# Keys of both heads of a forgetting pair turned together, their low parts multiplied over 64 partitions

## The chip, the core and the metric

The kernel runs on one core of a Trainium2 chip. TensorE (PE) multiplies; its weight loads (PEld) have a row of their own in the profile. VectorE (DVE), ScalarE (ACT) and GpSimd (POOL) work on tiles in on-chip memory, and SyncE (SP) issues most transfers. The metric is the time of one execution on the device in microseconds; lower is better.

## The reference

One layer of a hybrid decoder, for 1024 tokens of width 1024 in float32:

```python
xn = rmsnorm(x, attn_norm_g)
proj = jnp.einsum('bsd,de->bse', xn, w_in)
qa, ka, va, qb, kb, vb, f_logit = jnp.split(proj, IN_SPLITS, axis=-1)
...
out_a = swa_sinks_attention(qa, ka, va, sink_logits)     # 8 heads of 64, window 128, 2 key heads
qb = rmsnorm(qb.reshape(b, s, B_HEADS, HEAD_DIM), q_norm_b)
kb = rmsnorm(kb.reshape(b, s, B_HEADS, HEAD_DIM), k_norm_b)
log_f = jax.nn.log_sigmoid(f_logit + b_forget)
out_b = forgetting_attention(qb, kb, vb, log_f)          # 8 heads of 64, causal, logit += c[t] - c[s]
x = x + jnp.einsum('bse,ed->bsd', mixed, w_out)
hn = rmsnorm(x, mlp_norm_g)
x = x + jnp.einsum('bsf,fd->bsd', jnp.square(jax.nn.relu(jnp.einsum('bsd,df->bsf', hn, w_up))), w_down)
```

The change lies in the forgetting attention: the product of queries and keys, before the softmax, for 8 heads in 4 pairs.

## The kernel before

Float32 accuracy is had by splitting. A number is written as a high part, which the array multiplies exactly enough, and a low part, the rest; a product of two such numbers is made of high by high, high by low and low by high, each a matmul of its own. All matmuls go through one helper (line 73), splits through lines 77 to 80.

The program has five stages that overlap at their edges: the first projection (to about 45 us), the windowed attention of the eight a-heads (45 to about 172 us), the forgetting attention of the b-heads (scores from 179 to 410 us), the output projection, and the two large products of the feed-forward part (about 445 us to the end). While attention runs, TensorE is also given the projections of the pairs to come (tile ps) and, later, the output projection (tile po); these "fillers" are put in at fixed counts of finished score units (PACE).

A b-pair p has two heads. Its work is eight units, four for head 0 (units 0 to 3), four for head 1 (4 to 7); a unit takes two blocks of 128 queries, in the order ORDER_B = (0, 2, 1, 3). For each chunk of up to 512 keys, `scores_b` issues three matmuls into a tile spb:

- q1 by k1: over 128 partitions. q1 holds the head's 64 query features twice, the high parts in one half of the partitions and the low parts in the other; k1 holds the high parts of the keys in both halves. So one matmul gives high by high and low by high.
- q1 by k2: k2 has the low parts of the keys in the head's own half (rows 0 to 63 for head 0, 64 to 127 for head 1), and zeros in the other half, so that the low parts of the query add nothing. There are two such tiles, `k2_of[0]` for all heads 0 and `k2_of[1]` for all heads 1; POOL writes the zeros once, in pair 0.
- in the last chunk, the causal mask, a bf16 matmul of a 128x128 identity by the mask.

DVE then adds the bias cb and takes a running minimum (line 663), and ACT takes the exponential (line 669). `mix_b` turns the probabilities (tpb), splits them (pth, ptl) and multiplies by the values (pvb).

Queries and keys come from the projection with tokens on partitions, and are turned on TensorE by `turn` (line 302): four 128-token transposes into one tile of 512 columns. `make_q_b` turns both heads' queries at once (128 columns of features). `make_k_b` turns the keys of one head (64 columns), once for each half c of the tokens; `k_split` then copies them twice into k1 on ACT (lines 343, 344) and subtracts the low parts into k2 on DVE (line 346). The next pair's tiles are prepared during the current pair (`ahead`): queries at unit 4, keys of head 0 at unit 5, values of head 0 at unit 6, keys of head 1 at unit 7.

Buffers of one tag are taken in turn: "q1" has four, "k1" two. A writer waits until the last reader of the tile that had the buffer is done. The a-heads' queries and keys use the same tags before.

Which instruction of several ready ones goes first on an engine is settled when the program is built, by priorities (`prep` raises them) and a simulated timeline; afterwards each engine has a fixed order.

Of the kernel before, what the change touches and what calls it, by code (L numbers as in the profile page):

```python
# [8 lines left out]
F32 = mybir.dt.float32  # L9
F32R = mybir.dt.float32r  # L10
BF16 = mybir.dt.bfloat16
AF = mybir.ActivationFunctionType
ALU = mybir.AluOpType
# [3 lines left out]
P = 128  # L17
D = 1024
S = 1024
KT = D // P  # L20
NT = S // P
HD = 64
# [33 lines left out]
def hybrid_layer(  # L56
# [13 lines left out]
    nc = tc.nc  # L70

    def mm(out, lhsT, rhs, start, stop):
        return nc.tensor.matmul(out, lhsT, rhs, start=start, stop=stop)  # L73
# [8 lines left out]
    def rsqrt(pool, out, t, shape, tag):  # L82
# [15 lines left out]
        out=ident, in_=ident, pattern=[[-1, P]], compare_op=ALU.not_equal,  # L98
# [17 lines left out]
    for i in range(2):  # L116
        nc.vector.tensor_tensor(
            out=gqk[:, i : i + 1], in0=vec[:, 2 * i : 2 * i + 1],
            in1=vec[:, 2 * i + 1 : 2 * i + 2], op=ALU.mult,
# [25 lines left out]
    ap2 = at.enter_context(tc.tile_pool(name="ap2", bufs=1, side="right"))  # L145
# [5 lines left out]
        out=maskd, in_=maskd, pattern=[[-1, P]], compare_op=ALU.is_ge,  # L151
# [23 lines left out]
    for k in range(KT):  # L175
# [10 lines left out]
        for cs in halves:  # L186
            nc.scalar.activation(xh[:, k, cs], xr[:, cs], AF.Copy, scale=ga[:, k : k + 1])
            last_x = nc.vector.scalar_tensor_tensor(
                out=xl[:, k, cs], in0=xr[:, cs], scalar=ga[:, k : k + 1],
                in1=xh[:, k, cs].bitcast(F32), op0=ALU.mult, op1=ALU.subtract,  # L190
# [102 lines left out]
    def q_split(hi, lo, src, gain):  # L293
        nc.scalar.activation(hi, src, AF.Copy, scale=gain)
        nc.vector.scalar_tensor_tensor(
            out=lo, in0=src, scalar=gain, in1=hi.bitcast(F32), op0=ALU.mult, op1=ALU.subtract
        )

    def turn(x, col, w, c, name):
        pt = pa.tile([P, 512], F32, tag="tr", name=name, bufs=3)  # L300
        for j in range(4):
            nc.tensor.transpose(  # L302
                pt[:w, j * P : (j + 1) * P], x[:, 4 * c + j, col : col + w], ident
            )
        return pt
# [3 lines left out]
    def paced():  # L309
        return tc.issue_after(marks[-1]) if marks else nullcontext()  # L310

    qa, va = {}, []
    rows_of = [slice(h * HD, (h + 1) * HD) for h in range(2)]

    def tiles_q_a(g, c):
        for j in range(2):
            qa[g, j, c] = ap2.tile([P, 2, 512], F32R, tag="q1", name=f"q1a{g}{j}", bufs=4)

    def make_q_a(g, c, j):
        x, col = (((q0, 0), (q3, 0)), ((q3, P), (q3, 2 * P)))[g][j]  # L320
# [4 lines left out]
            q_split(q1[r, h, :], q1[ro, h, :], pt[r, :], gqk[r, 0:1])  # L325

    def make_q_b(x, p):
        q1 = [ap2.tile([P, S], F32R, tag="q1", name=f"q1b{p}{h}", bufs=4) for h in range(2)]
        for c in range(2):
            cs = slice(c * 512, (c + 1) * 512)  # L330
            pt = turn(x, 0, P, c, "ptq")
            for h in range(2):
                r, ro = rows_of[h], rows_of[1 - h]
                q_split(q1[h][r, cs], q1[h][ro, cs], pt[r, :], gqk[r, 1:2])
        return q1
# [2 lines left out]

    k2_of = [ap2.tile([P, S], F32R, name=f"k2z{i}") for i in range(2)]

    def k_split(k1, i, src, cs, both):
        r, ro = rows_of[i], rows_of[1 - i]
        nc.scalar.copy(k1[r, cs], src)
        nc.scalar.copy(k1[ro, cs], src)
        for rr in (r, ro) if both else (r,):
            nc.vector.tensor_tensor(
                out=k2_of[i][rr, cs], in0=src, in1=k1[r, cs].bitcast(F32), op=ALU.subtract
            )

    k1a = {}  # L350

    def make_k_a(x, col, c):
        cs = slice(c * 512, (c + 1) * 512)
        pt = turn(x, col, P, c, "ptk")
        for g in range(2):
            if c == 0:
                k1a[g] = ap2.tile([P, S], F32R, tag="k1", name=f"k1a{g}", bufs=2)
            k_split(k1a[g], g, pt[rows_of[g], :], cs, True)

    def make_k_b(x, col, p, h):  # L360
        k1 = ap2.tile([P, S], F32R, tag="k1", name=f"k1b{p}{h}", bufs=2)
        if p == 0:
            nc.gpsimd.memset(k2_of[h][rows_of[1 - h], :].bitcast(F32), 0.0)
        for c in range(2):
            cs = slice(c * 512, (c + 1) * 512)
            pt = turn(x, col + h * HD, HD, c, "ptk")
            k_split(k1, h, pt[:HD, :], cs, False)
        return k1

    def evict_pt(pt, cols):  # L370
        hi = ap2.tile([P, 512], F32R, tag="pth", name="pth", bufs=3)
# [10 lines left out]
    for t in range(NT):  # L382
# [4 lines left out]
        out=rt, in0=rt, scalar1=1.0 / D, scalar2=EPS, op0=ALU.mult, op1=ALU.add  # L387
# [6 lines left out]
    for t in range(0, NT, 4):  # L394
# [8 lines left out]
        out=dist, in_=dist, pattern=[[-1, 256]], compare_op=ALU.is_ge, fill=BIG,  # L403
# [3 lines left out]
        out=dist, in_=dist, pattern=[[1, 256]], compare_op=ALU.is_ge, fill=BIG,  # L407
# [8 lines left out]
    for pattern, base, sign in (  # L416
# [5 lines left out]
            out=before, in_=before, pattern=pattern, compare_op=ALU.is_ge, fill=0.0,  # L422
# [56 lines left out]
    def start_a():  # L479
        for c in range(2):  # L480
            tiles_q_a(0, c)
        for t in range(2):
            wa1_tile(t)
        for c in range(2):
            wa1_tile(2 + c)
            with tc.issue_after(middle[-1]):
                prep(make_k_a, q0, P, c)
            prep(make_q_a, 0, c, 0)
        for g in range(2):
            va.append(split_v(q0[:, :, 256 + g * HD : 256 + (g + 1) * HD], f"va{g}"))  # L490
        prep(make_q_a, 0, 0, 1)
        for t in range(4, NT):
            wa1_tile(t)
        prep(make_q_a, 0, 1, 1)
# [128 lines left out]
    heads = {}  # L623

    def prep_q(p):
        heads[p, "q"] = make_q_b(qkb[p], p)

    def prep_k(p, h):
        heads[p, "k1", h] = make_k_b(qkb[p], P, p, h)
        if h == 0:  # L630
            load_c(p, 0)

    def load_c(p, h):
        cb = heads[p, "cb", h] = ap2.tile([P, S], F32, tag="bias", name=f"cb{p}{h}", bufs=2)
        nc.sync.dma_start(cb, c_d[2 * p + h].partition_broadcast(P))
# [3 lines left out]
        heads[p, "v", h] = split_v(qkb[p][:, :, c0 : c0 + HD], f"vb{p}{h}")  # L639

    def scores_b(p, qp, h):
        q1, k1, k2, cb = heads[p, "q"][h], heads[p, "k1", h], k2_of[h], heads[p, "cb", h]
        probs = []
        for i in (2 * qp, 2 * qp + 1):
            nk = (i + 1) * P
            pr = ap2.tile(
                [P, S if i > 3 else 512], F32, tag="s" if i > 3 else "u", name="sb",
                bufs=NS if i > 3 else NU,
            )
            nm = ap3.tile([P, 4], F32, tag="nm", name="nmb", bufs=4)  # L650
            dn = ap3.tile([P, 4], F32, tag="dn", name="dnb", bufs=4)
            qs = q1[:, i * P : (i + 1) * P]
            for c in range((nk + 511) // 512):
                n = min(512, nk - c * 512)
                ne = max(n, 256)
                ks = slice(c * 512, c * 512 + ne)
                sp = pa.tile([P, 512], F32, tag="sc", name="spb", bufs=2)
                last = (c + 1) * 512 >= nk
                mm(sp[:, :ne], qs, k1[:, ks], True, False)
                mm(sp[:, :ne], qs, k2[:, ks], False, not last)  # L660
                if last:
                    pe = mm(sp[:, n - P : n], ident_b, mask_b, False, True)
                nc.vector.tensor_tensor_reduce(
                    out=pr[:, c * 512 : c * 512 + n], in0=sp[:, :n],
                    in1=cb[:, c * 512 : c * 512 + n], scale=1.0,
                    scalar=3e38 if c == 0 else nm[:, 0:1],
                    op0=ALU.add, op1=ALU.min, accum_out=nm[:, c : c + 1],
                )
            nc.scalar.activation(
                pr[:, :nk], pr[:, :nk], AF.Exp, scale=-1.0, bias=nm[:, c : c + 1],  # L670
                accum_out=dn_b[p % 2][:, h, i : i + 1] if p < 3 else dn[:, 0:1],
            )
            probs.append(pr)
            if p < 3:
                continue
            nc.vector.reciprocal(dn[:, 1:2], dn[:, 0:1])
            if i > 1:
                nc.vector.tensor_scalar_mul(pr[:, :nk], pr[:, :nk], dn[:, 1:2])
            else:
                nc.gpsimd.tensor_tensor(  # L680
                    out=pr[:, :nk], in0=pr[:, :nk],
                    in1=dn[:, 1:2].to_broadcast([P, nk]), op=ALU.mult,
                )
        marks.append(pe.ins)
        return probs
# [46 lines left out]
    qkb = {}  # L732
# [24 lines left out]
    def ahead(p, u):  # L757
        if p > 3:
            return
        if u == 4:  # L760
            prep(prep_q, p)
        if u == 5:
            prep(prep_k, p, 0)
        if u == 6:
            prep(prep_v, p, 0)
        if u == 7:
            prep(prep_k, p, 1)
# [155 lines left out]
    rr = o["zr"].tile([P, S], F32, name="rr")  # L923
# [334 lines left out]
    for i in range(len(STEPS)):  # L1258
        down(i)
        if STEPS[i][0] == len(PHASES) - 1 and late:  # L1260
            name, dt, cs = late.pop(0)
# [63 lines left out]
```

## Time and profile before

| | us |
|---|---|
| median of 3 runs | 1100.29 (1097.19 to 1101.08) |
| profiled execution, its own time | 1097.17 |
| its span | 1095.5 |
| TensorE busy in the span | 1081.4 |
| DVE, ACT, POOL busy | 774.7, 571.6, 365.2 |

The span goes from the first to the last instruction; the profiled execution's own time also holds what lies around it. A matmul's row in the timeline gives its start and its whole latency, and matmuls overlap, so what one costs is the distance from its start to the next one's start, not its length. The same goes for weight loads. A tile named 128*64 in such a row uses 128 rows and 64 columns of the array; the form behind it is the output.

### The profile page before, as it was taken

What the parts mean: (1) busy time and instruction counts of PE and PEld (TensorE: products, weight loads), DVE (VectorE), ACT (ScalarE), POOL (GpSimd) and SP (SyncE); (2) the same over time, 40 slices, a digit from 0 to 9 for tenths busy, and PEclk for the clock granted to TensorE, in tenths of its full rate; (3) what the DMA queues carried; (4) which work ended last, traced back from release to release, by engine and by line L of the source; (5) the groups of instructions that cost most, each with busy time, mean ns of one, the idle gap of its engine ahead of it and who ended that gap; (6) DMA issues with size and microseconds to landing.
All of it is one profiled execution on the core that took longest, in us unless ns stands there. A gap on an engine that the chain in (4) does not pass through costs nothing.

```text
span 1095.5 us, 15678 instructions
## 1 busy us (share of the span) xinstructions
PE 1081.4 (99%) x5557; PEld 934.0 (85%) x5557; DVE 774.7 (71%) x1327; ACT 571.6 (52%) x1013; POOL 365.2 (33%) x352
## 2 busy tenths in 40 slices
PE   9999999999998999999999999999999999999998
PEld 8999999999996888778888888888888888888886
DVE  8377677766777883898686869765665867674395
ACT  5558588676767764554545454443633433333331
POOL 5672523435433564223223232332222222222100
PEclk9999999999999999999999999999999999999999
DMA  8401212334347457663554443344898876665423
GB/s 301 146 23 52 71 38 61 115 93 149 116 154 279 156 174 280 228 214 127 195 194 177 172 165 143 144 173 144 311 391 312 306 288 230 233 224 186 174 91 115
DMA packets 96079, 195.69 MB, mean 179 GB/s; under 512 B 7376, under 2 KB 19584, under 8 KB 96000
## 3 DMA queue, kind: packets, MB, share of 16 engines
q1 hardware_dynamic: 95856, 194.66, 50.9%
q8 instruction: 44, 0.72, 0.3%
q14 instruction: 35, 0.29, 0.1%
q10 hardware_dynamic: 144, 0.02, 0.0%
HBM read 141.61 MB, written 53.04 MB: 178 GB/s over the span
## 4 chain that ended last, share of the span: by engine, by line
PE 86%; DVE 6%; DMA 5%; issue 1%; ACT 1%; POOL 1%; SPq 0%; ACTq 0%; DVEq 0%
PE pd L73 27%; PE pu L73 27%; PE ps L73 13%; PE po L73 5%; PE spb L73 3%; PE pvb L73 3%; PE tpb L705 3%; DMA xr<-in_xT_dram 1%; PE sp L73 1%; PE pv L73 1%; DMA xq<-in_x_dram 1%; PE tpa L534 1%; DMA h_d<-h 1%; PE ptk L302 1%; DVE bl L80 1%
## 5 line engine op out<-in xcount | busy, mean ns | idle before, releaser
L73 PE MATMUL pd<-hx,wx 128*128 128x512 f32 (+1 forms) x1350 | 304.9, 388 | 0.0
L73 PEld LDWEIGHTS pd<-hx,wx 128*128 128x128 f32 x1350 | 252.7, 188 | 52.2
L73 PE MATMUL pu<-bh,wu 128*128 128x512 f32 x896 | 276.5, 390 | 1.1 <-ACT wu L77 1.1
L73 PEld LDWEIGHTS pu<-bh,wu 128*128 128x128 f32 x896 | 168.2, 188 | 36.6 <-ACT wu L77 1.6
L73 PE MATMUL ps<-w,xh 128*128 128x384 f32 (+1 forms) x640 | 176.0, 345 | 0.7 <-DVE z L431 0.6
L73 PE MATMUL pu<-bl,wu 128*128 128x512 f32 x448 | 174.5, 390 | 0.6 <-DVE bl L80 0.6
L77 ACT CAST hx<-hr 128x1024 fp32r<-128x1024 f32 x56 | 58.9, 1052 | 176.6 <-PE pd L73 170.6
L80 POOL TENSOR_TENSOR wx<-wda,wx 128x1024 fp32r<-128x1024 f32 x24 | 64.5, 2686 | 196.4 <-ACT wx L77 169.1
L80 DVE TENSOR_TENSOR hx<-hr,hx 128x1024 fp32r<-128x1024 f32 x56 | 72.3, 1299 | 72.4 <-ACT hx L77 72.4
L73 PEld LDWEIGHTS ps<-w,xh 128*128 128x128 f32 x640 | 115.3, 189 | 3.1 <-DVE z L431 1.0
L73 PE MATMUL ps<-w,xl 128*128 128x384 f32 (+1 forms) x320 | 109.8, 344 | 0.0
L73 PEld LDWEIGHTS pu<-bl,wu 128*128 128x128 f32 x448 | 84.1, 188 | 19.2 <-DVE bl L80 1.0
L73 PE MATMUL po<-mix,wos 128*128 128x512 f32 x384 | 94.0, 395 | 1.0 <-ACT wos L77 0.7
L80 POOL TENSOR_TENSOR wu<-wus,wu 128x512 fp32r<-128x512 f32 x32 | 47.2, 1476 | 127.2 <-ACT wu L77 127.2
L73 PEld LDWEIGHTS po<-mix,wos 128*128 128x128 f32 x384 | 70.4, 188 | 15.5 <-ACT wos L77 1.1
L80 POOL TENSOR_TENSOR wu<-wur,wu 128x512 fp32r<-128x512 f32 x32 | 43.3, 1354 | 88.7 <-ACT wu L77 88.7
L77 ACT CAST wu<-wus 128x512 fp32r<-128x512 f32 x64 | 38.4, 618 | 58.8 <-PE pu L73 55.1
L374 DVE TENSOR_TENSOR ptl<-tpb,pth 128x512 fp32r<-128x512 f32 (+1 forms) x80 | 49.3, 631 | 25.1 <-ACT pth L373 23.1
L999 DVE TENSOR_TENSOR ht<-hb 128x512 f32<-128x512 f32 x32 | 21.8, 722 | 63.2 <-ACT hb L1054 63.2
L80 POOL TENSOR_TENSOR w<-wr,w 128x384 fp32r<-128x384 f32 (+1 forms) x47 | 51.5, 1106 | 41.2 <-ACT w L77 29.3
L77 ACT CAST wx<-wda 128x1024 fp32r<-128x1024 f32 x56 | 58.2, 1044 | 6.7 <-DMA wda<-in_w_d_dram 6.6
L73 PEld LDWEIGHTS ps<-w,xl 128*128 128x128 f32 x320 | 60.3, 188 | 1.0
(214 smaller groups left out, 1935.9 us busy)
## 6 DMA issues: line engine op xcount, KB each, us to landing
wda<-in_w_d_dram SPq DMA_DIRECT2D x34, 1024.0 KB, 9.0
hr<-hid_d SPq DMA_DIRECT2D x56, 512.0 KB, 6.0
wur<-in_w_u_dram SPq DMA_DIRECT2D x32, 512.0 KB, 4.3
hid_d<-ht SPq DMA_DIRECT2D x16, 1024.0 KB, 4.3
hid_d<-hb SPq DMA_DIRECT2D x16, 768.0 KB, 3.6
mix<-mixs_d SPq DMA_DIRECT2D x7, 1024.0 KB, 7.4
wr<-in_w_b_dram SPq DMA_DIRECT2D x32, 192.0 KB, 2.5
xr<-in_xT_dram SPq DMA_DIRECT2D x16, 256.0 KB, 4.8
```

The lines of the kernel that those rows point to most:

```text
L73: return nc.tensor.matmul(out, lhsT, rhs, start=start, stop=stop)
L77: hi_eng.copy(hi, src)
L80: lo_eng.tensor_tensor(out=lo, in0=src, in1=hi.bitcast(F32), op=ALU.subtract)
L302: nc.tensor.transpose(pt[:w, j * P : (j + 1) * P], x[:, 4 * c + j, col : col + w], ident)
L374: nc.vector.tensor_tensor(out=lo[:, cols], in0=pt[:, cols], in1=hi[:, cols].bitcast(F32), op=ALU.subtract)
L534: nc.tensor.transpose(tp[:, hh * P : (hh + 1) * P], pts[hh // 2][:, hh % 2, c0 : c0 + P], ident)
L705: nc.tensor.transpose(tp[:, c0 : c0 + P], probs[qi][:, kb * P : (kb + 1) * P], ident)
L999: eng.tensor_tensor(out=out, in0=a, in1=b, op=ALU.subtract)
```

## The change

For pairs 1 to 3, the keys of both heads are turned together, 128 columns of features at a time, one half of the tokens at unit 5 and the other half at unit 7. Pair 0 keeps one head at a time. The low parts of both heads of a pair now stand in one tile, `k2_of[p % 2]`, head 0 in rows 0 to 63 and head 1 in rows 64 to 127; the zeros are gone, and the q1 by k2 matmul runs over the 64 partitions of the head, for queries and keys alike. The tags "q1" and "k1" are replaced by six named places, q0 to q5, and a table QK says in which places a pair's two query tiles and two key tiles stand.

```diff
+    QK = ((0, 1, 4, 5), (2, 3, 0, 4), (1, 5, 2, 0), (3, 4, 1, 2))
+
+    def qk1(i, shape, name):
+        return ap2.tile([P] + shape, F32R, tag=f"q{i}", name=name, bufs=1)
...
-        q1 = [ap2.tile([P, S], F32R, tag="q1", name=f"q1b{p}{h}", bufs=4) for h in range(2)]
+        q1 = [qk1(QK[p][h], [S], f"q1b{p}{h}") for h in range(2)]
...
-    def k_split(k1, i, src, cs, both):
+    def k_split(k1, k2, i, src, cs, both):
...
-                out=k2_of[i][rr, cs], in0=src, in1=k1[r, cs].bitcast(F32), op=ALU.subtract
+                out=k2[rr, cs], in0=src, in1=k1[r, cs].bitcast(F32), op=ALU.subtract
...
-    def make_k_b(x, col, p, h):
-        k1 = ap2.tile([P, S], F32R, tag="k1", name=f"k1b{p}{h}", bufs=2)
-        if p == 0:
-            nc.gpsimd.memset(k2_of[h][rows_of[1 - h], :].bitcast(F32), 0.0)
-        for c in range(2):
-            cs = slice(c * 512, (c + 1) * 512)
-            pt = turn(x, col + h * HD, HD, c, "ptk")
-            k_split(k1, h, pt[:HD, :], cs, False)
-        return k1
+    def make_k_b(x, col, p, c, hs):
+        cs = slice(c * 512, (c + 1) * 512)
+        if len(hs) == 2:
+            pt = turn(x, col, P, c, "ptk")
+        else:
+            pt = turn(x, col + hs[0] * HD, HD, c, "ptk")
+        for h in hs:
+            if (p, "k1", h) not in heads:
+                heads[p, "k1", h] = qk1(QK[p][2 + h], [S], f"k1b{p}{h}")
+            src = pt[rows_of[h] if len(hs) == 2 else rows_of[0], :]
+            k_split(heads[p, "k1", h], k2_of[p % 2], h, src, cs, False)
...
-    def prep_k(p, h):
-        heads[p, "k1", h] = make_k_b(qkb[p], P, p, h)
-        if h == 0:
+    def prep_k(p, u):
+        if p == 0:
+            for c in range(2):
+                make_k_b(qkb[p], P, p, c, (u,))
+        else:
+            make_k_b(qkb[p], P, p, u, (0, 1))
+        if u == 0:
             load_c(p, 0)
...
-        q1, k1, k2, cb = heads[p, "q"][h], heads[p, "k1", h], k2_of[h], heads[p, "cb", h]
+        q1, k1, cb = heads[p, "q"][h], heads[p, "k1", h], heads[p, "cb", h]
+        k2, r = k2_of[p % 2], rows_of[h]
...
-                mm(sp[:, :ne], qs, k2[:, ks], False, not last)
+                mm(sp[:, :ne], qs[r], k2[r, ks], False, not last)
```

How the order moves is seen at two places. The first is TensorE at the end of pair 0 and the beginning of pair 1 (in these rows qkb is the projected input that is turned into ptk; q1b and k1b are queries and keys, and k2z is the tile of low parts; the form is the output's). Before:

```order
L73 MATMUL spb<-k1b_2876,q1b_2741 128x256
L73 MATMUL spb<-k2z_441,q1b_2741 128x256
L73 LDWEIGHTS ident_b
L73 MATMUL spb<-mask_b,ident_b 128x128
L73 MATMUL ps<-w,xh 128x384
L302 MATMUL ptk<-ident,qkb_1767 64x128 x4
L73 MATMUL spb<-k1b_2876,q1b_2741 128x512
L73 MATMUL spb<-k2z_441,q1b_2741 128x512
L73 MATMUL ps<-w,xl 128x384
```

With the change:

```order
L73 MATMUL spb<-k1b_2879,q1b_2739 128x256
L73 MATMUL spb<-k2z_442,q1b_2739 128x256
L73 LDWEIGHTS ident_b
L73 MATMUL spb<-mask_b,ident_b 128x128
L73 MATMUL ps<-w,xh 128x384
L73 MATMUL ps<-w,xl 128x384
L302 MATMUL ptk<-ident,qkb_1767 128x128 x4
L73 MATMUL spb<-k1b_2879,q1b_2739 128x512
L73 MATMUL spb<-k2z_442,q1b_2739 128x512
L73 MATMUL ps<-w,xh 128x384 x2
```

The turned keys are 128 rows high instead of 64, pair 1's low parts stand in the other k2 tile, and every k2z matmul still stands by itself, between a k1b matmul and the mask or a filler. Before, the group of four turns head 1's first half; now it turns both heads' second half, and four more 64-row transposes that followed within 20 rows are gone.

The second place is ACT at the same time, where pair 1's keys are copied (sb are the scores under the exponential, mtb and qkb evictions of products, pth the turned probabilities, mixn a part of the mixed output). Before, k1b_2876 is head 0 and k1b_3091 head 1:

```order
L373 CAST pth<-tpb 128x384
L343 CAST k1b_3091<-ptk 64x512
L344 CAST k1b_3091<-ptk 64x512
L77 CAST mixn<-mixr 128x512
L669 ACTIVATE sb,dn_b_90<-sb,nmb 128x256
L616 COPY qkb_2559<-ps 128x384
L343 CAST k1b_3091<-ptk 64x512
L344 CAST k1b_3091<-ptk 64x512
```

With the change, k1b_2879 is head 0 and k1b_2883 head 1:

```order
L685 ACTIVATE sb,dn_b_90<-sb,nmb 128x256
L350 CAST k1b_2879<-ptk 64x512
L351 CAST k1b_2879<-ptk 64x512
L77 CAST mixn<-mixr 128x512
L350 CAST k1b_2883<-ptk 64x512
L351 CAST k1b_2883<-ptk 64x512
L382 CAST pth<-tpb 128x512
```

The late copies, which belonged to head 1 alone, are now the second half of the tokens of both heads. Their number and shape are the same.

More of the change, by code (lines that the diff above doesn't have):

```diff
@@ L316, in tiles_q_a @@
         for j in range(2):
-            qa[g, j, c] = ap2.tile([P, 2, 512], F32R, tag="q1", name=f"q1a{g}{j}", bufs=4)
+            qa[g, j, c] = qk1(2 * c + j, [2, 512], f"q1a{g}{j}")
     def make_q_a(g, c, j):
@@ L356, in make_k_a @@
             if c == 0:
-                k1a[g] = ap2.tile([P, S], F32R, tag="k1", name=f"k1a{g}", bufs=2)
-            k_split(k1a[g], g, pt[rows_of[g], :], cs, True)
-    def make_k_b(x, col, p, h):
-        k1 = ap2.tile([P, S], F32R, tag="k1", name=f"k1b{p}{h}", bufs=2)
-        if p == 0:
-            nc.gpsimd.memset(k2_of[h][rows_of[1 - h], :].bitcast(F32), 0.0)
-        for c in range(2):
-            cs = slice(c * 512, (c + 1) * 512)
-            pt = turn(x, col + h * HD, HD, c, "ptk")
-            k_split(k1, h, pt[:HD, :], cs, False)
-        return k1
+                k1a[g] = qk1(4 + g, [S], f"k1a{g}")
+            k_split(k1a[g], k2_of[g], g, pt[rows_of[g], :], cs, True)
+    def make_k_b(x, col, p, c, hs):
[9 more added lines that the diff above has]
+            k_split(heads[p, "k1", h], k2_of[p % 2], h, src, cs, False)
     def evict_pt(pt, cols):
```

## The prediction

> **What bounds the kernel now.** I read the page's busy line and its chain of waits first, then the stretch in which the changed code runs, then who makes TensorE wait there.
>
> ```profile
> PE 1081.4 (99%) x5557; PEld 934.0 (85%) x5557; DVE 774.7 (71%) x1327; ACT 571.6 (52%) x1013; POOL 365.2 (33%) x352
> ...
> PE 86%; DVE 6%; DMA 5%; issue 1%; ACT 1%; POOL 1%; SPq 0%; ACTq 0%; DVEq 0%
> ```
>
> TensorE (PE) is occupied for 99% of the span and holds 86% of the chain that ends last. The scores of the forgetting heads, tile spb, show where the change acts (duration in ns as min/median/max, then the first and last start in us):
>
> ```profile
> L73 PEld LDWEIGHTS spb<-k2z,q1b x96: 187/190/201, 180.2 to 409.8; 128*128 128x128 f32 x96
> L73 PE MATMUL spb<-k2z,q1b x96: 274/376/477, 180.2 to 409.9; 128*128 128x512 f32 x48, 128*128 128x256 f32 x32, 128*128 128x384 f32 x16
> ```
>
> So the stretch is 172 to 425 us. Its busy times (length, then PE, PEld, DVE, ACT, POOL, the granted clock), and the longest waits of the weight loads in it (us, times, longest):
>
> ```profile
> 172.00:425.00 253.00, 249.73 (x1598) 225.37 (x1597) 180.40 (x439) 175.90 (x387) 116.20 (x154) 1.00 0.47 153
> ```
>
> ```profile
> PEld L73 <- issue: 6.2, 29, 0.3
> PEld spb L73 <- DVE nmb L663: 2.6, 4, 1.1
> PEld pvb L73 <- DVE mtb L722: 1.2, 1, 1.2
> ```
>
> PE is busy 249.73 of 253.00 us at a granted clock of 1.00; DVE has 73 us free, ACT 77, POOL 137. The weight loads wait for another engine's result 3.8 us in these rows. Whatever an edit adds to PE's own row there lengthens the program nearly one for one, and what it takes from the other engines gains next to nothing. The case is therefore decided by matmul time.
>
> **The change part by part.** *Fewer turnings.* The order of the changed program has 24 key transposes fewer: for pairs 1 to 3, 48 of 64 columns become 24 of 128 columns. The timeline of PE around one group of four, and at four transposes of 128 columns (start and length in us):
>
> ```profile
> 172.13 0.51 PE L73 MATMUL ps<-w,xh 128*128 128x384 f32 x2
> 172.48 0.60 PE L302 MATMUL ptk<-ident,qkb 128*64 128x128 f32 x4
> 172.83 0.43 PE L73 MATMUL ps<-w,xl 128*128 128x384 f32 x1
> 173.09 0.52 PE L73 MATMUL ps<-w,xh 128*128 128x384 f32 x2
> 173.46 0.34 PE L73 MATMUL ps<-w,xl 128*128 128x384 f32 x1
> 173.63 0.52 PE L73 MATMUL ps<-w,xh 128*128 128x384 f32 x2
> ...
> 187.47 0.60 PE L534 MATMUL tpa<-ident,sa 128*128 128x128 f32 x4
> 187.82 0.42 PE L73 MATMUL ps<-w,xh 128*128 128x384 f32 x1
> ```
>
> The group starts at 172.48 and its follower at 172.83, which is 0.35 us; the follower then holds its place until 173.09, 0.26 us where such a matmul later takes 0.17 (173.46 to 173.63). Together 0.35 + 0.09 = 0.44 us, 0.11 us for one. A 128-column transpose costs the same: the four tpa take 0.35 us again. Gain: 24 x 0.11 = **2.6 us**.
>
> *The low parts over 64 partitions.* The number of these matmuls (96) and their columns stay; only the rows of the array that they use are halved, for the weights and for the moving keys. This is how such a pair runs now, first PE, then the weight loads:
>
> ```profile
> 188.08 0.39 PE L73 MATMUL spb<-k1b,q1b 128*128 128x512 f32 x1
> 188.31 0.40 PE L73 MATMUL spb<-k2z,q1b 128*128 128x512 f32 x1
> 188.55 0.33 PE L73 MATMUL ps<-w,xh 128*128 128x384 f32 x1
> ```
>
> ```profile
> 188.09 0.19 PEld L73 LDWEIGHTS spb<-k2z,q1b 128*128 128x128 f32 x1
> 188.32 0.19 PEld L73 LDWEIGHTS ps<-w,xh 128*128 128x128 f32 x1
> ```
>
> Each load begins 0.01 us after the matmul ahead of it has started and lies wholly under it; matmuls follow every 0.23 us. Does that survive when the matmul in the middle uses 64 rows? The kernel has one place with a 64-row matmul between 128-row ones: the offsets of the forget gates, tile off. PE, then its loads, then DVE:
>
> ```profile
> 125.70 0.34 PE L73 MATMUL ps<-w,xh 128*128 128x384 f32 x1
> 125.97 0.27 PE L73 MATMUL off<-cum,before 64*64 64x1 f32 x2
> 126.17 0.66 PE L534 MATMUL tpa<-ident,sa 128*128 128x128 f32 x4
> ```
>
> ```profile
> 125.53 0.19 PEld L73 LDWEIGHTS ps<-w,xh 128*128 128x128 f32 x1
> 125.97 0.19 PEld L73 LDWEIGHTS off<-cum,before 64*64 64x64 f32 x2 [0.25 <-issue]
> 126.17 0.53 PEld L534 LDWEIGHTS tpa<-ident,sa 128*128 128x128 f32 x5
> ```
>
> ```profile
> 122.23 0.41 DVE L462 TENSOR_TENSOR_SCAN cum<-ones,ptf 64x128 f32<-64x128 f32 x1 [2.35 <-PE ptf L460]
> 126.28 0.15 DVE L472 COPY offs<-off 64x1 f32<-64x1 f32 x1 [2.16 <-PE off L73]
> ```
>
> The load for off should have started with the matmul at 125.70. It started at 125.97, behind 0.25 us in which the load row stood still for no semaphore ("issue"); its input cum was done at 122.64. The matmul ahead, at the pace of 0.17, was through at 125.87: **0.10 us** more went by. On the way out the same: two loads of 0.13 us took 0.19 together, so the second began 0.06 after the first and was in place about 126.08; the first 128-row load came at 126.17, **0.10 us** later. Between the two 64-row matmuls there is no such pause. A narrower matmul with all rows pays nothing, as the transpose of 64 columns shows, whose load is ahead in the usual way:
>
> ```profile
> 121.74 0.34 PE L73 MATMUL ps<-w,xl 128*128 128x384 f32 x1
> 121.92 0.27 PE L460 MATMUL ptf<-ident,zt 128*64 128x128 f32 x1
> 121.94 0.60 PE L73 MATMUL ps<-w,xh 128*128 128x384 f32 x2
> ```
>
> ```profile
> 121.74 0.11 PEld L460 LDWEIGHTS ptf<-ident,zt 128*64 128x64 f32 x1
> ```
>
> So it is the rows. I read it as: a load for another number of rows waits until the array has emptied, 0.10 us, and then isn't hidden. The Trainium skill's page TensorEngine Tiling (Array Packing), section Key Properties, says that a change of the tiling mode drains the TensorE; off agrees (0.10 us each way), while ptf, whose 128x64 is a mode of its own on that page, shows no drain.
>
> Two more rows, the loads of off as a group and one load for the mask matmul:
>
> ```profile
> L73 PEld LDWEIGHTS off<-cum,before x2: 129/131/133, 126.0 to 126.0; 64*64 64x64 f32 x2
> ```
>
> ```profile
> 321.14 0.10 PEld L73 LDWEIGHTS <-ident_b 128*128 128x128 bf16 x1 [0.16 <-issue]
> ```
>
> What a load costs in the open: an off load has 131 ns and hands over after 0.06 (0.19 for both, less 0.13), so some 0.08 us of a row is lag; a k2 load of 190 ns then holds the array for 0.11 us.
>
> In the changed program's order all 96 k2 matmuls stand alone between 128-row ones, so there are 192 switches. Going in: 96 x (0.10 + 0.11) = 20.2 us. Coming out, 58 have the mask matmul behind them, whose bf16 load isn't ahead today either (0.16 us of issue in front of it), so only the pause is new: 58 x 0.10 = 5.8 us. The other 38 have a matmul or transpose whose load then stands in the open: 38 x 0.21 = 8.0.
>
> Sum **34.0 us**. Bounds: below, nothing at all (if off's pause were something else); with the pauses alone 192 x 0.10 = 19.2; above, each load open for its whole row: 96 x 0.29 + 5.8 + 38 x 0.29 = 44.7 us. I take 34.0, since off is the only 64-row case and gives both the pause and the hand-over.
>
> ```profile
> L343 ACT CAST k1b<-ptk x16: 564/580/581, 174.7 to 362.3; 64x512 fp32r<-64x512 f32 x16
> ...
> L346 DVE TENSOR_TENSOR k2z<-ptk,k1b x16: 674/683/685, 175.9 to 364.6; 64x512 fp32r<-64x512 f32 x16
> ```
>
> *What is hidden.* The two POOL memsets of k2's other half go, in POOL's free time. ACT copies and DVE subtractions keep number and shape (64x512). In named places pair 1 to 3's keys are written over tiles last read in unit 3, at units 5 and 7, so ACT no longer waits for the last scores of the pair before. The second half of head 0's keys, however, is turned only at unit 7: for pair 1 its first user stands 35 matmuls and transposes behind in PE's order, 0.11 us or more each, so 3.9 us, and two ACT copies and a subtraction take 2 x 0.58 + 0.68 = 1.8 us. It is covered; uncovered it would cost up to 1.8 us three times.
>
> A slower PE gives the others time: of the 3.8 us of waits above I let 2 go.
>
> **Sum.** The profiled execution took 1097.17 us (span 1095.5 and 1.7 around it): 1097.2 - 2.6 + 34.0 - 2.0 = 1126.6. The median of the three runs, 1100.29, lies 3.1 above that execution, the lowest run on it; I add 1 for that: **1127.6 us**, 2.5% slower than the median.
>
> **The rivals.** *Only the pauses cost, the loads stay hidden* (12%): 1097.2 + 19.2 - 2.6, less up to 3.8 of waits: 1110.0 to 1113.8. For it: a load of half the rows might be let in early; against it, off's load wasn't. *A 64-row matmul is free* (12%): only the transposes count, 1094.6, within 0.5% of before. For it: off is one place with a single moving column, in another number format. Here the Trainium skill speaks the other way, too: its page TensorE: Matmul & The Clock Gate, section Why this matters for your kernels, says that a matmul over few rows takes the same time as one over 128. No row here shows such a matmul of 512 columns. *Faster* (4%): free 64-row matmuls and, beyond that, named places that take away the 3.3 us in which PE isn't busy in the stretch (253.00 - 249.73): 1097.2 - 2.6 - 3.3 = 1091.3. Against it: the longest of these waits are for DVE's running minimum nmb and for mtb, which the change doesn't touch. The forecast has the remaining 72%. That the change doesn't do what it says is ruled out by the order, in which the 24 transposes and both memsets are gone.
>
> **How the numbers follow.** The range takes the forecast with its upper bound (1097.2 - 2.6 + 44.7 + 1 = 1140.3) and below it the rival of pauses alone (1110, and 3 us for the runs' own spread): 84% of the chance, less some tails. The two cases at 1095 and below stay out. Runs of this kernel differ by up to 0.35% (1097.19 to 1101.08), so 0.5% is about what can be told from no change: faster 0.04, same 0.12, slower 0.84.
>
> **What would show it.** Right: loads for k2 start about 0.10 us after the matmul ahead is through instead of 0.01 after its start; k1 to k2 at 512 columns takes 0.44 us instead of 0.23; "issue" in front of these loads grows from 6.2 us to above 20; the stretch lengthens from 253 to some 280 us and nothing before 172 or after 445 does. Wrong: k2's loads still begin under the matmul ahead, or the lost time stands in front of other tiles (k1b waiting for ACT, pvb for DVE).

## The result and the profile after

| | before | changed |
|---|---|---|
| median | 1099.21 (5 runs, 1097.19 to 1101.08) | 1131.69 (5 runs, 1129.63 to 1133.47) |
| ratio | | 1.0289, 95% interval 1.0272 to 1.0306 |
| profiled execution, span | 1095.5 | 1130.0 |

The changed kernel is 32.5 us slower. The prediction had 1127.6 us and 84% for slower. Its total held, in part by luck: two of its terms were off in opposite directions, by some 3 us and by 6 to 7, and a third one, for the clock, was missing. The rest of the document is about that.

The busy line and the chain of waits of the changed kernel:

```profile
PE 1113.9 (99%) x5533; PEld 938.1 (83%) x5533; DVE 777.3 (69%) x1327; ACT 573.8 (51%) x1013; POOL 364.0 (32%) x350
...
PE 92%; DVE 4%; DMA 2%; ACT 1%; POOL 1%; issue 1%; SPq 0%; DVEq 0%; ACTq 0%
```

PE has 24 instructions fewer and is busy 32.5 us longer; DVE, ACT and POOL work as long as they did, to within 3 us. The tile view for spb, the low-part matmuls and their loads (ns as min/median/max, first and last start in us):

```profile
L73 PEld LDWEIGHTS spb<-k2z,q1b x96: 182/183/285, 180.6 to 439.7; 64*128 64x128 f32 x96
L73 PE MATMUL spb<-k2z,q1b x96: 379/490/792, 180.6 to 439.7; 64*128 64x512 f32 x48, 64*128 64x256 f32 x32, 64*128 64x384 f32 x16
```

The median matmul went from 376 to 490 ns, and the last one starts 30 us later. One pair in the timeline, PE first and then its weight loads:

```profile
341.99 0.40 PE L73 MATMUL spb<-k1b,q1b 128*128 128x512 f32 x1
342.32 0.49 PE L73 MATMUL spb<-k2z,q1b 64*128 64x512 f32 x1
342.75 0.23 PE L73 MATMUL spb<-mask_b,ident_b 128*128 128x128 bf16 x1
342.79 0.42 PE L73 MATMUL ps<-w,xl 128*128 128x384 f32 x1
```

```profile
341.82 0.19 PEld L73 LDWEIGHTS spb<-k1b,q1b 128*128 128x128 f32 x1
342.32 0.18 PEld L73 LDWEIGHTS spb<-k2z,q1b 64*128 64x128 f32 x1 [0.31 <-issue]
342.74 0.10 PEld L73 LDWEIGHTS <-ident_b 128*128 128x128 bf16 x1 [0.24 <-issue]
```

The k1 matmul streams its 512 columns in 0.23 us (341.99 to 342.22); k2's load begins 0.10 us after that, where it began with the k1 matmul before. The k2 matmul then holds the array for 0.43 us instead of 0.24: its own load lies in the open inside that time, and the mask's load starts only at its end, at 342.74. Among the waits of the weight loads from 172 to 480 us (us, times, longest), the first two rows are "issue", a wait for no semaphore. The row of 6.2 us before was that of the mask's loads, which have no tile name, and is 6.9 now; the 21.5 us in front of spb's loads are new:

```profile
PEld spb L73 <- issue: 21.5, 82, 0.5
PEld L73 <- issue: 6.9, 31, 0.4
...
PEld po L73 <- DMA mix<-mixs_d: 3.0, 1, 3.0
PEld pvb L73 <- DVE mtb L738: 2.1, 2, 1.2
...
PEld spb L73 <- DVE nmb L679: 0.7, 2, 0.4
```

Something else is new. The windows of the changed kernel around three places (length, busy PE, PEld, DVE, ACT, POOL with counts, granted clock, DMA share, GB/s):

```profile
352.80:356.20 3.40, 2.34 (x11) 1.41 (x11) 3.34 (x11) 1.83 (x6) 0.00 (x0) 1.00 1.03 417
356.20:363.00 6.80, 6.80 (x24) 4.63 (x22) 2.68 (x9) 3.77 (x9) 3.19 (x4) 0.50 1.03 408
363.00:369.80 6.80, 6.61 (x44) 5.04 (x44) 5.35 (x12) 5.16 (x10) 1.74 (x5) 1.00 0.34 129
458.60:462.00 3.40, 0.65 (x3) 0.57 (x4) 1.95 (x5) 1.19 (x3) 0.57 (x3) 1.00 0.99 395
462.00:465.40 3.40, 3.40 (x10) 2.63 (x9) 0.00 (x0) 0.00 (x0) 0.00 (x0) 0.50 1.02 415
496.10:499.50 3.40, 1.33 (x6) 0.75 (x4) 1.33 (x3) 1.53 (x3) 0.84 (x1) 1.00 0.82 247
499.50:506.30 6.80, 6.10 (x14) 4.78 (x15) 6.80 (x8) 2.50 (x5) 3.42 (x3) 0.50 0.76 253
```

TensorE runs at a granted clock of 0.50 for 17.1 us in all, at the seam of pairs 2 and 3 and in the output projection; 24 matmuls pass in 6.8 us there, 44 in the 6.8 us behind. The profiled execution of the kernel before has no such stretch until its last few us. Each of the three half-clock stretches stands behind 3.4 us in which few matmuls ran (11, 3 and 6), because PE waited for mtb, for mix or for wos.

Where the feed-forward part stands, before in the first view, the changed kernel in the second:

```profile
L73 PE MATMUL pu<-bh,wu x896: 387/389/793, 476.9 to 785.7; 128*128 128x512 f32 x180
...
L73 PE MATMUL pd<-hx,wx x1350: 278/389/389, 786.0 to 1090.6; 128*128 128x512 f32 x192, 128*128 128x256 f32 x1
```

```profile
L73 PE MATMUL pu<-bh,wu x896: 389/389/793, 514.1 to 820.3; 128*128 128x512 f32 x180
...
L73 PE MATMUL pd<-hx,wx x1350: 278/389/389, 820.5 to 1125.1; 128*128 128x512 f32 x192, 128*128 128x256 f32 x1
```

It begins 37.2 us later and ends 34.5 later: the whole loss arises before it, and 2.7 us come back in it.

### The profile page after: what moved, and what is told of

Read it like the earlier page. It is cut to its first block, busy times and chain, and to the rows that moved or that the text cites. A ratio compares the mean times of both kernels' runs of the same rounds, so it can differ in the third digit from the quotient of the medians.

```text
span 1130.0 us, 15629 instructions
## 1 busy us (share of the span) xinstructions
PE 1113.9 (99%) x5533; PEld 938.1 (83%) x5533; DVE 777.3 (69%) x1327; ACT 573.8 (51%) x1013; POOL 364.0 (32%) x350
## 4 chain that ended last, share of the span: by engine, by line
PE 92%; DVE 4%; DMA 2%; ACT 1%; POOL 1%; issue 1%; SPq 0%; DVEq 0%; ACTq 0%
PE pu L73 27%; PE pd L73 27%; PE ps L73 13%; PE po L73 6%; PE spb L73 6%; PE pvb L73 3%; PE tpb L721 3%; PE qps L73 2%; PE sp L73 1%; PE pv L73 1%; PE tpa L543 1%; DMA mix<-mixs_d 1%; PE ptq L302 1%; DMA wr<-in_w_a_dram 1%; DVE k2z L353 0%
## 5 line engine op out<-in xcount | busy, mean ns | idle before, releaser
L73 PE MATMUL po<-mix,wos 128*128 128x512 f32 x384 | 99.6, 411 | 5.5 <-DMA mix<-mixs_d 2.8
L73 PEld LDWEIGHTS po<-mix,wos 128*128 128x128 f32 x384 | 73.4, 197 | 22.3 <-ACT wos L77 3.2
L685 ACT ACTIVATE sb<-sb,nmb 128x128 f32<-128x128 f32 (+3 forms) x64 | 49.7, 777 | 25.3 <-DVE nmb L679 25.2
```

Of the source, the lines that this page charges most:

```text
L685: nc.scalar.activation(pr[:, :nk], pr[:, :nk], AF.Exp, scale=-1.0, bias=nm[:, c : c + 1], accum_out=dn_b[p % 2][:, h, i : i + 1] if p < 3 ...
```

## The experiments

The theory in all of them: a 64-row matmul alone between 128-row ones pays a pause on each side and an open load, and this is the loss. Rivals: the loss comes from the keys turned together (A), or each 64-row matmul costs by itself, not each visit to 64 rows (B); later ones are named where they come up. Each ratio is to runs of the kernel before on the same chip (medians 1098.93 to 1099.49 us). One table first, since the readings rest on it. "Waits" sums the idle time of the weight loads from 40 to 520 us that another engine or a transfer ended. "Half clock" is the time at a granted clock of 0.50 before the last few us. "Rest" is the span less the waits and less half of the half-clock time, which is the most that time can have cost. Each row is one execution, the profiled one, which is not always close to the median of its kernel (halves early: 1099.66 us, median 1104.01), so differences of 2 us or so between rows mean little by themselves.

| kernel | 64-row visits | span | waits | half clock | rest |
|---|---|---|---|---|---|
| before | 0 | 1095.5 | 12.7 | 0 | 1082.8 |
| places only | 0 | 1095.7 | 12.9 | 0 | 1082.8 |
| full rows | 0 | 1100.1 | 20.2 | 0 | 1079.9 |
| full rows, halves early | 0 | 1098.0 | 18.3 | 0 | 1079.7 |
| before with 64 rows | 96 | 1126.9 | 11.0 | 3.4 | 1114.2 |
| changed | 96 | 1130.0 | 12.2 | 17.1 | 1109.3 |
| two halves | 102 | 1128.6 | 10.3 | 10.2 | 1113.2 |
| grouped | 66 | 1117.0 | 12.5 | 13.7 | 1097.6 |
| 72 visits, seam full | 72 | 1120.5 | 16.1 | 3.4 | 1102.7 |
| 72 visits, early full | 72 | 1114.0 | 13.0 | 0 | 1101.0 |

**Full rows.** The changed kernel, but with k2 over all 128 partitions. Since both halves of the tile are filled now, the product gains the low part of the query times the low part of the other head's keys; it is there to keep the form of the matmul, not its value.

```diff
-                mm(sp[:, :ne], qs[r], k2[r, ks], False, not last)
+                mm(sp[:, :ne], qs, k2[:, ks], False, not last)
```

> The changed kernel, with one edit: the low-part matmul runs over all 128 partitions of the shared k2 tile again (queries and keys unsliced). It then also adds the product of the head's low query parts and the other head's low keys, a term of the size of the low-by-low products that the kernel leaves out anyway. Theory (switching to 64 rows and back costs 0.10 us of pause each way and opens the weight loads): all 96 visits are gone, 24 transposes fewer stay: 2.6 us below the kernel before, 1094 to 1098 us. Rival A (turning both heads together, late second halves of the keys, or the named places make the loss): 1120 us or more still. Rival B (64-row matmuls slow in themselves): as the theory; e3 and e4 part them.

Measured: 1103.63 us (1101.64 to 1104.78), 1.0033 of before (1.0022 to 1.0044). Of the 32.5 us, 28.1 go with the 64 rows, so A falls as the main cause. But the theory wanted less than 1098: with the transposes saved and nothing else changed in the matmuls, the kernel is slower than before, not faster. In the tile view the matmuls are as they were before:

```profile
L73 PE MATMUL spb<-k2z,q1b x96: 276/378/483, 186.2 to 418.3; 128*128 128x512 f32 x48, 128*128 128x256 f32 x32, 128*128 128x384 f32 x16
```

The waits of its weight loads from 172 to 480 us:

```profile
PEld spb L73 <- DVE nmb L679: 4.3, 6, 1.8
PEld po L73 <- ACT wos L77: 2.7, 2, 2.3
PEld po L73 <- ACT mtb L737: 2.2, 1, 2.2
PEld po L73 <- POOL wos L80: 1.4, 3, 0.7
PEld pv L73 <- ACT pth L382: 1.2, 1, 1.2
...
PEld spb L73 <- DVE k2z L353: 0.2, 1, 0.2
```

The same view of before has 2.6 us for nmb, none for mtb by ACT and 1.1 for wos. The rest in the table is 2.9 us lower than before, which is the forecast gain of the transposes (2.6); the waits are 7.5 us higher. The gain came, and more than it was given back in front of other tiles. Over the whole span instead of 40 to 520 us the picture is the same: the waits rise by 7.3 us (16.1 to 23.4).

**Before with 64 rows.** The kernel before, with only its k2 matmul narrowed; the zeros are still written, but no longer read.

```diff
+        r = rows_of[h]
...
-                mm(sp[:, :ne], qs, k2[:, ks], False, not last)
+                mm(sp[:, :ne], qs[r], k2[r, ks], False, not last)
```

> The kernel before, with one edit: the low-part matmul takes only the head's 64 partitions of queries and of k2; the zeros are still written, keys are turned head by head, buffers by tags as before. Theory: all of the loss, without the 2.6 us that fewer transposes bring: 32 to 36 us above the kernel before, 1131 to 1136 us. Rival A (turning together or the places): no loss, 1097 to 1101 us.

Measured: 1128.32 us (1126.04 to 1129.96), 1.0257 (1.0241 to 1.0273), 28.8 above before. The 64 rows cost the same with and without the common turning (28.8 and 28.1). Both came out 3 to 4 us under the forecast's 34.0 less 2.0.

**Two halves.** The changed kernel with each k2 matmul cut into two column halves. If each 64-row matmul paid, the cost would double; if each visit pays, nothing changes but a few visits that the new order parts (102 instead of 96).

```diff
+                for x in (0, ne // 2):
+                    kx = slice(c * 512 + x, c * 512 + x + ne // 2)
+                    mm(sp[:, x : x + ne // 2], qs[r], k2[r, kx], False, not last and x > 0)
```

> The changed kernel with each low-part matmul split into two of half the columns: 192 matmuls over 64 rows instead of 96, in 102 visits instead of 96 (87 of them hold two). Theory (the visit costs, not the matmul): the second load stands under the first matmul, as between the two off matmuls; 32 pairs of 128 columns and 16 of 192 are shorter than a load of 0.11 us, some 2.5 us, and 6 more visits 2 us: 1133 to 1138 us. Rival B (each 64-row matmul costs 0.3 us more, whatever stands beside it): 96 more of them, 1155 to 1165 us.

Measured: 1130.95 us (1130.34 to 1132.36), 1.0284 (1.027 to 1.0298), 2 us below the range of the theory: 96 matmuls and loads more for nothing. In its timeline:

```profile
204.06 0.40 PE L73 MATMUL spb<-k1b,q1b 128*128 128x512 f32 x1
204.38 0.50 PE L73 MATMUL spb<-k2z,q1b 64*128 64x256 f32 x2
204.81 0.50 PE L73 MATMUL pv<-pth,va 128*128 128x512 f32 x1
```

Two halves hold the array for 0.43 us, as one whole did above. The second half's load is hidden: the switch costs, not the 64 rows, and B falls.

**Grouped.** The changed kernel, with both k1 matmuls of a block first and both k2 behind them, so that two k2 often stand together: 66 visits for 96 matmuls.

```diff
-                mm(sp[:, :ne], qs, k1[:, ks], True, False)
-                mm(sp[:, :ne], qs[r], k2[r, ks], False, not last)
...
+                k1m = mm(sp[:, :ne], qs, k1[:, ks], True, False)
+            for c, (n, ne, ks, sp) in enumerate(sps):
+                with tc.issue_after(k1m.ins):
+                    k1m = mm(sp[:, :ne], qs[r], k2[r, ks], False, c < len(sps) - 1)
```

> The changed kernel with the order of a query block's matmuls changed: where a block has two chunks of keys, both high-part matmuls come first and both low-part matmuls follow each other; 96 low-part matmuls in 66 visits. Theory (the visit costs about 0.35 us): 30 visits fewer, 9 to 11 us below the changed kernel, 1120 to 1125 us, with a few us either way from the later first chunk. Rival B (the matmul costs, not the visit): as the changed kernel, 1129 to 1134 us.

Measured: 1117.38 us (1115.68 to 1118.76), 1.0154 (1.0138 to 1.0169), 14.3 below the changed kernel and 3 below the range of the theory. In the timeline:

```profile
223.05 0.59 PE L73 MATMUL spb<-k1b,q1b 128*128 128x512 f32 x2
223.58 0.61 PE L73 MATMUL spb<-k2z,q1b 64*128 64x512 f32 x2
224.12 0.23 PE L73 MATMUL spb<-mask_b,ident_b 128*128 128x128 bf16 x1
```

Two k2 side by side take 0.54 us, where two alone would take 0.86. Between the two profiled executions lie 13.0 us, of which by the table 11.7 are in the rest, somewhat more than 30 visits at 0.3 us (9); the excess isn't resolved further. Grouped like this the kernel stays above before's time, since 66 visits remain.

**Places only.** Why do the waits grow under full rows? First suspect P: the named places. The kernel before with the table QK and the places q0 to q5, nothing else.

```diff
-        q1 = [ap2.tile([P, S], F32R, tag="q1", name=f"q1b{p}{h}", bufs=4) for h in range(2)]
+        q1 = [qk1(QK[p][h], [S], f"q1b{p}{h}") for h in range(2)]
...
-        k1 = ap2.tile([P, S], F32R, tag="k1", name=f"k1b{p}{h}", bufs=2)
+        k1 = qk1(QK[p][2 + h], [S], f"k1b{p}{h}")
```

> The kernel before, with the named places alone: six places q0 to q5 and the table QK for queries and keys; keys are turned head by head over 64 columns, the low parts stand in two tiles by head with zeros, all matmuls over 128 rows. The run with full rows lay 4 us above the kernel before where 2.6 below were forecast. Theory P (the places, or the order that comes out of them, make these waits): 1102 to 1105 us. Theory T (turning both heads together makes them, by its late second half or by the order that it leads to): 1097 to 1100 us, as the kernel before.

Measured: 1100.45 us (1097.41 to 1102.54), 1.0008 (0.9997 to 1.0018). The places cost nothing that can be told, and the waits are 12.9 us as before. P falls; the common turning (T) remains, and with it the tile of low parts that both heads share, which no run parts from it.

**Full rows, halves early.** Is it the second half of the keys, which comes as late as unit 7? In "full rows", that half is turned at unit 6 and the values of head 0 are made at unit 7 in its stead.

```diff
-            prep(prep_v, p, 0)
-        if u == 7:
             prep(prep_k, p, 1)
+        if u == 7:
+            prep(prep_v, p, 0)
```

> The changed kernel with the low-part matmuls over all 128 rows (as in the run with full rows, with the same small extra term) and the second halves of both heads' keys turned at unit 6, ahead of the values of head 0, which move to unit 7. Theory T-late (the late second half holds up the next pair's second unit): 1095 to 1099 us. Theory T-order (waits at the seam with the output projection, which no key is part of): 1100 to 1105 us, as with the second halves at unit 7.

Measured: 1104.01 us (1099.66 to 1106.12), 1.0039 (1.0025 to 1.0053), no better than full rows. The row for k2z of 0.2 us above stands at 186.2 us, in pair 0, whose keys are still turned head by head. So lateness of the second half is out. (In this kernel's trace the first scores of pair 3, at 346.8 us, wait 1.6 us for the ACT copy of that pair's first half, k1b L351.) Whether the new places of the instructions in the order make the waits, or PE's earlier arrival does, these runs don't tell; that stays open.

**72 visits, two ways.** The half clocks were the last question: are they a cause of their own beside the visits, and what triggers them? Both kernels give 24 of the 96 matmuls all 128 rows, those of two heads, once on both sides of the seam of pairs 2 and 3, where the first half clock stands, and once early.

```diff
-        k2, r = k2_of[p % 2], rows_of[h]
+        k2, r = k2_of[p % 2], slice(0, P) if (p, h) in ((2, 1), (3, 0)) else rows_of[h]
```

> The changed kernel with head 1 of pair 2 and head 0 of pair 3 (24 of 96 low-part matmuls, those around 345 to 365 us, where the changed kernel's profile shows TensorE's granted clock at one half for 6.8 us) over 128 rows, with the small extra term; the other 72 over 64 rows. Theory (each visit costs about 0.33 us in the array; where visits and waits crowd, the array does too little in a window of 3.4 us and the clock is halved behind it): 24 x 0.33 = 7.8 us less and no half clock near 356, another 2 to 3.4 us: 1120 to 1123 us. Rival (the half clock comes from something else, such as the switch of the stage): half clock there still, 1123 to 1126 us.

Measured: 1123.75 us (1122.29 to 1125.17), 1.0232 (1.0215 to 1.0249), 7.9 below the changed kernel and in the rival's range. A half clock of 3.4 us is still there, at 354.2 us, though the nearest 64-row matmul ahead of it is at 342.4: the waits at the seam are enough for it. By the table its waits are 3.9 us longer than the changed kernel's, which takes back part of what the visits gave.

The early one has ((0, 1), (1, 0)) in that line.

> The same for head 1 of pair 0 and head 0 of pair 1 (24 of 96, from about 215 to 270 us, where the clock was never halved). Theory: 7.8 us less by the visits, the half clock near 356 stays: 1123 to 1126 us. If the cost weren't proportional to the number of visits, both runs would lie off these times by the same amount.

Measured: 1116.57 us (1115.72 to 1117.29), 1.0162 (1.0147 to 1.0177), 15.1 below the changed kernel, where 7.8 were expected for 24 visits. The profiled execution has no half clock before its end. Its seam, 3.4 us with few matmuls and then what follows:

```profile
345.80:349.20 3.40, 2.58 (x13) 1.69 (x13) 2.81 (x10) 1.89 (x6) 0.41 (x1) 1.00 1.03 420
349.20:356.10 6.90, 6.37 (x37) 4.37 (x36) 4.40 (x10) 4.74 (x11) 3.48 (x8) 1.00 1.02 401
```

The 24 visits at 0.3 us (7.2) and the changed kernel's half clocks (at most 8.5 of their 17.1 us) make 15.7. So up to 8.5 of the changed kernel's 32.5 us are half clock, and they hang on where its waits happen to fall.

They hang on the execution, too, and the record lets one estimate what they cost. The five executions of the changed kernel took 1127.9 and 1128.7 us of span at a mean granted clock of 0.995 and 0.996, and 1130.0, 1131.1 and 1131.8 at 0.991, 0.991 and 0.990. Twice the span times what the clock lacks of 1 is the time at half clock: the second group had some 11 us more of it and took 2.7 us longer, a quarter of a us for each us and not half a us. The other kernels' executions give 0.1 to 0.5. At a quarter, an estimate, the 17.1 us cost some 4 us and not 8.5; then 3 to 4 of the 15.1 us here stay unexplained, and a visit comes to more in the changed kernel (below).

## Why the prediction was right, and where it was not

From the rows of the table, changed against before in spans, with the half clock at its most: 29.4 (the rest of the changed kernel less that of full rows) for the visits, -2.9 for the transposes, +8.5 at most for the half clock, -0.5 for the waits, which makes 34.5, the difference of the spans. Since the rest is what is left over, the sum itself proves nothing. What bears it out: the two kernels without a change in matmuls agree (1082.8 twice), the two with full rows agree (1079.9 and 1079.7), and the visits come out alike, within 0.06 us, in all kernels that have them, below.

- *What bounds the kernel.* Right: TensorE's own row does. The gaps around the k2 matmuls grew by some 31 us (below), and 28.1 and 28.8 us of added time came out.
- *Fewer turnings, -2.6.* This is the step that failed, not in its size (the rest fell by 2.9) but in taking the gain as one that reaches the end. With 128 rows the waits took 7.5 us more and the kernel was 4.1 us slower (full rows, against before's 1099.49 beside it); with 64 rows, 3.4 us slower (changed against "before with 64 rows"), there, by the table, through more half clock (at most 8.5 against 1.7 us). The prediction counted the waits for other engines, 3.8 us, but didn't ask what becomes of these waits when PE comes to them earlier or in another order. Which of the two it was stays open.
- *Low parts over 64 partitions, 34.0.* The mechanism was right, the term too large: 28.1 and 28.8 measured. By visit it was 0.35 us; the table gives 0.31 in the changed kernel (29.4 / 96), 0.33 in "before with 64 rows" (31.4 / 96) and in two halves (33.3 / 102), 0.32 and 0.29 with 72 visits, 0.27 in grouped (17.7 / 66). Waits over the whole span instead give 0.26 to 0.32; a quarter of the half clock instead of half of it gives 0.29 to 0.35, with 0.35 in the changed kernel, so how much too large the term was hangs on that price. The timeline doesn't. It shows all three parts: a pause ahead of the load, a load in the open, a pause behind. Each piece was taken a little too large. As medians over the 512-column pairs in the timelines, k1 to k2 went from 0.235 to 0.327 us and k2 to the mask from 0.238 to 0.431, so a pause is 0.09 us instead of 0.10 and the open load 0.10 instead of 0.11; a follower other than the mask adds 0.105 for its own load. (Where k1 follows the mask or a transpose, its own load lies in the open even with all rows, and k1 to k2 goes from 0.32 to 0.41 us: the same 0.09 more.) That makes 58 x 0.285 + 38 x 0.39 = 31 us in these gaps, of which 28 to 29 reach the end.
- *Waits, -2.0.* They fell by 0.5. The slower PE did give others time within the scores (nmb 2.6 to 0.7 us), but the output projection took it back. Its rows in the waits of the weight loads, before from 405 to 478 us, then the changed kernel from 440 to 515:

```profile
PEld po L73 <- ACT wos L77: 1.1, 1, 1.1
...
PEld po L73 <- DMA mix<-mixs_d: 0.5, 1, 0.5
```

```profile
PEld po L73 <- ACT wos L77: 3.2, 1, 3.2
PEld po L73 <- DMA mix<-mixs_d: 3.0, 1, 3.0
```

- *Clock.* The prediction read 1.00 in the stretch and has no term for it. The changed kernel's profiled execution spends 17.1 us at 0.50, which cost 4 us by the estimate above and 8.5 at most.
- *Late second half, covered.* Right: in the changed kernel nothing on TensorE waits for k1b or k2z, and earlier halves change nothing. In the other kernels with common turning such waits are 0.2, 0.4 and 1.6 us, once each. *Named places at nothing:* right, 1.0008.
- *The signs.* Right: the load 0.10 us behind the end of the matmul ahead; issue from 6.2 to 21.5 and 6.9 us; scores that end 30 us later. Wrong: k1 to k2 was to take 0.44 us and takes 0.33, with the load inside k2's own 0.43: the matmul and its load both bear the start 342.32. Wrong also: "nothing after 445 does". From the last score to the first pu went 66.9 us before (410.0 to 476.9) and 74.1 after (440.0 to 514.1).
- *The rivals.* Pauses alone would have been 1110 to 1114; the load does lie open. A 64-row matmul isn't free when it stands alone. The sentence of the Trainium skill that spoke for that rival (TensorE: Matmul & The Clock Gate, Why this matters for your kernels) holds within a run of such matmuls, as two halves shows, and not at their edges. The drain at a change of mode, which the Trainium skill has (TensorEngine Tiling (Array Packing), Key Properties), is borne out by the pauses of 0.09 us.

The time was missed by 4 us. The visits were forecast some 3 us too dear (34.0 less 2.0 against 28 to 29), and the turnings 6 to 7 us too good. That the one took back half of the other was luck.

## What to carry to other kernels

A matmul over 64 rows between matmuls over 128 cost about 0.3 us here, more than its 512 columns (0.23 us): leave zeros in the unused rows rather than cut them away, or put several 64-row matmuls in a row. A gain of 3 us on the bounding engine was taken back whole by its waits elsewhere, so before such a gain is booked, look at who the engine waits for next and how long. A difference of a few us between variants may be clock rather than work: look at the granted clock in windows before a step is blamed.

## What was not expected of the hardware

The array does not have to idle for the clock to fall. Apart from those at the very end, all half clocks in these profiles begin right behind a stretch of about 3.4 us with few matmuls, last 3.4, 6.8, 10.2 or 13.7 us, and in the changed kernel their starts lie whole multiples of 3.413 us apart (356.2, 462.0, 499.5: 31 and 11). The Trainium skill (TensorE: Matmul & The Clock Gate, Part 1: The HAM clock gate) has such free-running windows and half clock after an idle one. The measured windows were not idle. Two halves, ahead of and in its half clock:

```profile
353.40:356.80 3.40, 2.76 (x17) 2.00 (x17) 3.37 (x9) 1.98 (x4) 0.00 (x0) 1.00 1.02 420
356.80:367.00 10.20, 10.20 (x38) 7.50 (x37) 4.25 (x14) 4.31 (x11) 3.60 (x6) 0.50 0.99 391
```

PE is busy 2.76 of 3.40 us by its rows and still the clock is halved for 10.2 us. Full rows has a window with fewer matmuls and less busy time in it, and keeps its clock:

```profile
466.10:469.50 3.40, 1.54 (x8) 0.96 (x6) 1.64 (x2) 2.27 (x5) 1.28 (x2) 1.00 0.89 307
469.50:472.90 3.40, 3.11 (x13) 2.26 (x14) 3.40 (x5) 1.78 (x3) 1.89 (x2) 1.00 0.50 155
```

Counted by columns at the pace of full flow, the windows ahead of a half clock were filled to 0.16 to 0.44, and the emptiest without one to about 0.4 to 0.5 (an estimate from the matmuls' rows; where a kernel has no half clock, where its windows lie had to be inferred from the last fall at its end). So a badly filled window is what they have in common, but the two ranges meet, and no sharp limit can be read from these runs.
